# Context-mixer matrix products placed behind the expert picks on TensorE; the second tile's routing in quarters

## The chip, the core and the metric

The kernel runs on one NeuronCore of a Trainium2 chip. A core has a matrix engine (TensorE, PE in the rows; its weight loads are PEld), a vector engine (VectorE, DVE), an engine for activations (ScalarE, ACT), a general engine (GpSimd, POOL), and an engine that here only issues transfers (SyncE, SP). Each engine takes its instructions from its own queue in the order in which the compiled program put them. Transfers run on 16 DMA engines that all queues share. The metric is the device time of one launch in microseconds (us).

## The reference, cut to what matters

The input is one sequence of 256 rows of width 1024. A first block (three attention branches, then a "PEER" feed-forward) feeds a second block of two layers, each a mixer of a context (256 rows) and the latent rows, and a mixture of experts. The part around the change is the PEER feed-forward and the context's half of the second block's first mixer.

```python
q = (hf @ w_q).reshape(T, 8, 2, 128)
sc = einsum('thpd,hpkd->thpk', q, subkeys)
s1, i1 = top_k(sc[:, :, 0], 16);  s2, i2 = top_k(sc[:, :, 1], 16)
cand = s1[..., :, None] + s2[..., None, :]          # 16 x 16 per head
top_s, pos = top_k(cand, 16)                        # 16 of 16384 experts per head
gate = softmax(top_s)
act = gelu(einsum('chkd,cd->chk', u[ic], hc))       # per token 8 x 16 = 128 experts
out = einsum('chk,chkd->cd', gate * act, v[ic])
...
# second block, layer 0 (mLSTM mixer): context first, its state then feeds the latent rows
p = h_ctx @ w_in;  qk = silu(conv(p[q, k]));  v, o, gates = the rest of p
y = mlstm(q, k, v, gates);  y = norm(y) * sigmoid(o);  out_ctx = y @ w_out
```

The context's products do not depend on the PEER result, so they may run beside it.

## The kernel before

The 256 rows are two tiles of 128 tokens. `peer` (L1227) runs one phase with three strands.

- **Picks** (`picks`, L1276). For each tile, 128 picks, one for each of the 8 x 16 chosen experts; 256 in all. A pick is an indirect transfer issued by POOL (L1296) that fetches 128 rows of 8 KB (1 MB: the expert's u and v rows for every token) into one of RING = 6 buffers; a VectorE product with accumulation over 128x1024 (u times h2, through the helper at L608), and two TensorE products 128x512 in fp32 that add v, scaled by a diagonal matrix, into one accumulator. Two picks make a batch (BATCH = 2): the GELU, the product with the gate and two diagonals are made once for a batch (ACT, DVE), so TensorE gets four 128x512 products (helper `mm`, L611) for a batch. A ring buffer is free for its next pick when TensorE has read it.
- **Routing**. `prepare` (L1240) multiplies 8 slabs of `w_peer_q` for both tiles and routes tile 0 in pieces: `route(0, ...)` after slabs 0, 1, 3 and 7 (1, 1, 2 and 4 heads). `prepare_last` routes tile 1 in two pieces of four heads. `route` (L1334) is VectorE work: two rounds of maximum, index and replacement for each key list, then wide sums, comparisons and reductions over the heads of the piece.
- **Context**. `context_task` (L1519) streams 17 weight slabs (`in_w`, 1 MB each, SP, L558), each 48 products of 128x256 after a split of the slab into a high and a low part (ACT and DVE, L592 and L599), then the mixer's convolution, gates, 8 heads of attention (`mlstm_attend`, L1713), norms, output product, and the opening of the expert layer.

Emission order: `peer` chains the routing of tile 0 and then the context (with `prepare_last` woven in at a rate of 1.5) into one strand `side`. `drive` steps through the picks, and for every pick, which costs 2600, lets `side` run on for 2600 x PACE of its own cost units; a context slab costs 5200. With PACE = 0.21 a slab is emitted about every nine and a half picks. That is only the order of emission: a scheduler at build time then sets each engine's final order from the emission order and its own model of when operands are ready. `stream.shrink(2)` in `prepare` hands back two slots of the weight stream at slab 7, `stream.grow(1)` after the phase takes one again. `behind(i)` (L594) is there before: what is emitted inside it may not stand ahead of instruction `i` on that instruction's engine.

Of the kernel before, what the change touches and what calls it, by code (L numbers as in the profile page):

```python
# [23 lines left out]

PACE = 0.21

# [467 lines left out]
class K:  # L494
# [115 lines left out]
    def mm(self, ps, l, r, start=True, stop=True):  # L610
        self.nc.tensor.matmul(ps, l, r, start=start, stop=stop, skip_group_check=True)  # L611

# [614 lines left out]
    def peer(self):  # L1227
        h2, g = self.f(2048, True), self.bcast_row("ffn")
        self.ada_steps(99)
        self.mc = self.f(128, True)  # L1230
        h2T = self.norm_T([x.a for x in self.x], self.col("g_ffn"), sums=self.sq.a[:, :8], rows=(g, h2))
        self.sq.free(), g.free()
        self.mod_cols(0, [(n, b) for n in range(2) for b in range(2)])
        self.mod_cols(1, [(0, 0), (1, 0)])
        self.routes = [{"heads": 0, "rows": self.f(128), "gate": self.f(128), "act": self.f(128)} for _ in range(2)]
        side = self.chain((0.3 * c for c in self.prepare(h2T)), self.weave(self.context_task(), [self.prepare_last()], 1.5))
        self.drive(self.picks(h2, side), [side], PACE)
        self.stream.grow(1)

    def prepare(self, h2T):  # L1240
# [3 lines left out]
        for s in range(8):  # L1244
# [13 lines left out]
            p.free(), q.free()  # L1258
            yield 5200
            if s == 7:  # L1260
                for b in h2T:
                    b.free()
                sub.free()
                self.stream.shrink(2)
                self.units.lo = deque([None])
            if s in (0, 1, 3, 7):
                yield from self.route(0, {0: 0, 1: 1, 3: 2, 7: 4}[s], s + 1)

    def prepare_last(self):

        for h in (0, 4):
            yield from self.route(1, h, h + 4)
        for b in self.sc:
            self.stream.give_back(b)

    def picks(self, h2, prep):  # L1276
# [4 lines left out]
        for i, r in enumerate(self.routes):  # L1281
# [6 lines left out]
            for k in range(0, 128, BATCH):  # L1288
# [13 lines left out]
                for j, b in enumerate(got):  # L1302
# [3 lines left out]
                    for f in range(2):  # L1306
                        self.mm(po.a[:, f * 512:(f + 1) * 512], d, b[:, 1024 + f * 512:1024 + (f + 1) * 512], k + j == 0, k + j == 127)
            for f in range(2):
# [404 lines left out]
    def mlstm_attend(self, S, C):  # L1713
# [84 lines left out]

        ab = deque([alpha(0), alpha(1)])
        P = deque([weights(0, ab.popleft())])  # L1800
        for h in range(8):
            if h < 7:
                P.append(weights(h + 1, ab.popleft()))
            if h < 6:
                ab.append(alpha(h + 2))
            yield 5000 if lat else 2600
# [595 lines left out]
```

## Time and profile before

| | us |
|---|---|
| median of 3 runs (lowest, highest) | 2654.55 (2654.09, 2659.9) |
| profiled execution, its own time | 2645.13 |
| span of that execution, first to last instruction | 2643.4 |
| pick phase in it: first gather issued to last pick begun | 410.1 to about 1218 |
| mean granted TensorE clock (share of full speed) | 0.965 |

PE was busy for 87% of the span, DVE for 47%, ACT 29%, POOL 23%; the DMA engines moved 853 MB, 323 GB/s over the span. These shares are means over stages with different limits. The page's 40 slices (66 us each) show it: slices 7 to 18 are the pick phase, and in it the DMA digit stands at 9 with 405 to 420 GB/s in some slices, and at 8 or 9 with 306 to 350 GB/s in others. Rows that give busy times for chosen stretches are therefore read by stretch, each against the stretch's length. A busy number in such a row is in us; the count behind it is of recorded instructions (an fp32 product of 128x512 has two records, one of the context's 128x256 products one).

### The profile page before, as it was taken

To read this page: it belongs to the slowest core of one execution; us is meant where nothing else is said; L and a number is where in the kernel's file an instruction comes from. 1 tells how busy PE (TensorE), PEld (TensorE's weight loads), DVE (VectorE), ACT (ScalarE), POOL (GpSimd) and SP (SyncE) were. 2 spreads that over 40 slices of the span, in tenths; PEclk is the share of its full clock that TensorE was granted. 3 is DMA by queue.
4 is the path that set the end of the run, shared out by engine and by line. 5 is a ranking of instruction groups with operands and counts; after the bars stand their busy time and mean duration, and the time that the engine had idled before them with its cause. 6 is when DMAs were issued, how large, how long until landed. Compare 5 with 4: busy or idle time off the path is not lost.

```text
span 2643.4 us, 32351 instructions
## 1 busy us (share of the span) xinstructions
PE 2290.3 (87%) x12327; PEld 1386.1 (52%) x12327; DVE 1235.5 (47%) x2849; ACT 761.9 (29%) x1500; POOL 619.4 (23%) x517
## 2 busy tenths in 40 slices
PE   8999987788778897777888999999879989888876
PEld 7888985356323562225876344444469963222213
DVE  4465368899856774556774112211296451000001
ACT  6554343244513642113542000000233530000000
POOL 4233444334434433333420000000033310000000
PEclk9999998999999999999888999999979989999998
DMA  7676558888999889995456999999966389999998
GB/s 272 228 250 227 212 190 306 335 323 326 350 418 405 308 332 388 420 420 219 153 188 242 392 398 409 409 409 409 371 225 212 113 326 404 409 409 409 410 409 276
DMA packets 195323, 853.28 MB, mean 323 GB/s; under 512 B 14558, under 2 KB 39726, under 8 KB 148832
## 3 DMA queue, kind: packets, MB, share of 16 engines
q1 hardware_dynamic: 153376, 569.31, 56.6%
q0 software_dynamic: 41792, 281.90, 27.6%
q8 instruction: 97, 1.59, 0.2%
q14 instruction: 58, 0.48, 0.0%
HBM read 849.97 MB, written 1.18 MB: 322 GB/s over the span
## 4 chain that ended last, share of the span: by engine, by line
PE 49%; DMA 19%; DVE 14%; issue 8%; ACT 4%; POOL 4%; SPq 1%; POOLq 0%; DVEq 0%; ACTq 0%
PE pp L611 48%; DMA fa<-in_puv,fa 5%; DVE fa L608 5%; POOL fa L1296 3%; DMA fa<-in_moe_down 2%; ACT fa L592 2%; DMA rw<-in_moe_down 2%; DVE fa L599 2%; DMA rt<-in_moe_up 1%; DMA fa<-in_moe_up 1%; PE pp L621 1%; DMA rw<-in_moe_up 1%; DMA rw<-in_moe_gate 1%; DVE rw L599 1%; DMA fa<-in_moe_gate 1%
## 5 line engine op out<-in xcount | busy, mean ns | idle before, releaser
L611 PE MATMUL pp<-fa 128*128 128x512 f32 (+8 forms) x4900 | 1283.0, 492 | 222.7 <-ACT fa L592 157.9
L611 PEld LDWEIGHTS pp<-fa 128*128 128x128 f32 (+2 forms) x4900 | 555.7, 159 | 837.1 <-issue 432.7
L608 DVE SCALAR_TENSOR_TENSOR fa<-fa 128x1024 f32<-128x1024 f32 (+5 forms) x561 | 411.4, 756 | 166.7 <-DMA fa<-in_puv,fa 160.2
L611 PE MATMUL pp<-rw,rt 128*128 128x256 f32 x2928 | 399.9, 295 | 19.3 <-DVE rw L599 5.5
L611 PEld LDWEIGHTS pp<-rw,rt 128*128 128x128 f32 x2928 | 372.4, 197 | 42.3 <-issue 12.9
L1296 POOL DMA_INDIRECT fa<-in_puv,fa x256 | 274.3, 1072 | 450.7 <-PE pp L611 333.4
L592 ACT ACTIVATE fa<-fa 128x2 f32<-128x2 f32 (+9 forms) x477 | 189.9, 421 | 541.4 <-DVE fa L608 398.8
L611 PE MATMUL pp<-rt,rw 128*128 128x256 f32 x2448 | 327.7, 293 | 19.5 <-ACT rw L592 4.6
L611 PEld LDWEIGHTS pp<-rt,rw 128*128 128x128 f32 x2448 | 309.7, 197 | 36.5 <-issue 10.3
L599 DVE TENSOR_TENSOR fa<-pp,fa 128x512 f32<-128x512 f32 (+3 forms) x217 | 121.2, 565 | 440.3 <-PE pp L611 422.6
L592 ACT ACTIVATE fa<-pp 128x512 f32<-128x512 f32 (+4 forms) x164 | 93.8, 578 | 746.0 <-PE pp L611 586.2
L599 POOL TENSOR_TENSOR rw<-fa,rw 128x1024 fp32r<-128x1024 f32 x81 | 210.2, 2596 | 326.3 <-ACT rw L592 317.1
L592 ACT ACTIVATE rw<-fa 128x1024 fp32r<-128x1024 f32 x208 | 215.9, 1053 | 237.6 <-PE pp L611 132.2
L611 PE MATMUL pp<-rt,fa 128*64 128x512 f32 (+3 forms) x736 | 240.6, 574 | 16.1 <-DMA rt<-in_moe_up 7.8
L599 DVE TENSOR_TENSOR rw<-fa,rw 128x1024 fp32r<-128x1024 f32 x127 | 166.8, 1315 | 163.4 <-ACT rw L592 160.7
L611 PE MATMUL pp<-rw,fa 128*64 128x512 f32 (+2 forms) x720 | 202.4, 582 | 16.7 <-DMA rw<-in_moe_down 6.9
L605 DVE TENSOR_SCALAR fa<-pp,fa 128x128 f32<-128x128 f32 (+1 forms) x80 | 36.4, 460 | 254.7 <-PE pp L611 177.2
L599 DVE TENSOR_TENSOR fa<-fa 128x2 f32<-128x2 f32 (+11 forms) x325 | 99.4, 318 | 70.1 <-ACT fa L592 45.9
L611 PEld LDWEIGHTS pp<-rt,fa 128*64 128x64 f32 (+1 forms) x736 | 65.9, 124 | 118.0 <-issue 78.1
L611 PEld LDWEIGHTS pp<-rw,fa 128*64 128x64 f32 (+1 forms) x720 | 58.2, 124 | 128.8 <-issue 86.8
L621 PE MATMUL pp<-ct,fa 128*128 128x128 f32 (+3 forms) x425 | 73.7, 305 | 46.8 <-ACT fa L592 21.5
L592 ACT ACTIVATE fa<-ct,fa 128x128 f32<-128x128 f32 x256 | 88.8, 393 | 70.5 <-DVE fa L599 69.7
(136 smaller groups left out, 943.1 us busy)
## 6 DMA issues: line engine op xcount, KB each, us to landing
fa<-in_w SPq DMA_DIRECT2D x105, 1024.0 KB, 5.1
fa<-in_moe_gate SPq DMA_DIRECT2D x72, 1024.0 KB, 15.2
fa<-in_moe_down SPq DMA_DIRECT2D x68, 1024.0 KB, 14.1
fa<-in_moe_up SPq DMA_DIRECT2D x60, 1024.0 KB, 17.9
fa<-in_ada_w SPq DMA_DIRECT2D x48, 1024.0 KB, 5.4
rw<-in_moe_up SPq DMA_DIRECT2D x36, 1024.0 KB, 16.8
rt<-in_moe_down SPq DMA_DIRECT2D x31, 1024.0 KB, 13.3
rt<-in_moe_up SPq DMA_DIRECT2D x28, 1024.0 KB, 16.9
```

The source lines that it names most:

```text
L592: return self.nc.scalar.activation(out, in_, func, **kw)
L599: (eng or self.nc.vector).tensor_tensor(out, a, b, op=op)
L605: (eng or self.nc.vector).tensor_scalar(out, a, s1, s2, op0=op0, op1=op1, **kw)
L608: self.nc.vector.scalar_tensor_tensor(out, a, s, b, op0=op0, op1=op1, **kw)
L611: self.nc.tensor.matmul(ps, l, r, start=start, stop=stop, skip_group_check=True)
L621: self.nc.tensor.transpose(ps, x, self.c("ident")[:k, :k])
L1296: self.nc.gpsimd.indirect_dma_start(b, None, self.t["puv"], bass.IndirectOffsetOnAxis(ap=rows.bitcast(U32)[:, j:j + 1], axis=0))
```

## The change

1. `mm` returns its instruction. `picks` remembers in `self.pace` the last product of each batch, from the batch at which tile 0 has all its 8 heads routed, and all through tile 1. `peer` hands `drive` the generator `paced(side)`: each step of the side strand that `drive` takes is emitted inside `behind(self.pace)`, so its TensorE instructions stand behind the products of the batch they are emitted with. Other engines' queues are not bound by it.
2. `prepare_last` routes tile 1 in four pieces of two heads.
3. PACE goes from 0.21 to 0.2: a slab about every ten picks.
4. `stream.shrink(2)` moves from slab 7 to slab 3 of `prepare`.
5. `mlstm_attend`, for the context only: the decay rows (`alpha`) are fetched one head ahead instead of two, and `weights` of a head is emitted with the head itself, not one ahead. For the latent rows nothing changes (`lat` is 1).

```diff
-PACE = 0.21
+PACE = 0.2
...
     def mm(self, ps, l, r, start=True, stop=True):
-        self.nc.tensor.matmul(ps, l, r, start=start, stop=stop, skip_group_check=True)
+        return self.nc.tensor.matmul(ps, l, r, start=start, stop=stop, skip_group_check=True)
...
+        self.pace = None
         self.routes = [{"heads": 0, "rows": self.f(128), "gate": self.f(128), "act": self.f(128)} for _ in range(2)]
         side = self.chain((0.3 * c for c in self.prepare(h2T)), self.weave(self.context_task(), [self.prepare_last()], 1.5))
-        self.drive(self.picks(h2, side), [side], PACE)
+        self.drive(self.picks(h2, side), [self.paced(side)], PACE)
         self.stream.grow(1)
...
+            if s == 3:
+                self.stream.shrink(2)
             if s == 7:
                 for b in h2T:
                     b.free()
                 sub.free()
-                self.stream.shrink(2)
...
+    def paced(self, side):
+
+        while True:
+            with nullcontext() if self.pace is None else self.behind(self.pace):
+                c = next(side, None)
+            if c is None:
+                return
+            yield c
+
     def prepare_last(self):
 
-        for h in (0, 4):
-            yield from self.route(1, h, h + 4)
+        for h in range(0, 8, 2):
+            yield from self.route(1, h, h + 2)
...
                     for f in range(2):
-                        self.mm(po.a[:, f * 512:(f + 1) * 512], d, b[:, 1024 + f * 512:1024 + (f + 1) * 512], k + j == 0, k + j == 127)
+                        last = self.mm(po.a[:, f * 512:(f + 1) * 512], d, b[:, 1024 + f * 512:1024 + (f + 1) * 512], k + j == 0, k + j == 127)
+                if r is self.routes[1] or r["heads"] == 8:
+                    self.pace = last
...
-        ab = deque([alpha(0), alpha(1)])
-        P = deque([weights(0, ab.popleft())])
+        ab = deque(alpha(h) for h in range(2 if lat else 1))
+        P = deque([weights(0, ab.popleft())] if lat else [])
         for h in range(8):
-            if h < 7:
-                P.append(weights(h + 1, ab.popleft()))
-            if h < 6:
-                ab.append(alpha(h + 2))
+            if h + lat < 8:
+                P.append(weights(h + lat, ab.popleft()))
+            if h + lat < 7:
+                ab.append(alpha(h + lat + 1))
```

What this moves on the engines' queues, in the program's order. In these rows `fa 128x512` is a pick's product (two for each pick), `rw,rt 128x256` one of the context's products, `fa 128x129` and `fa 128x256` the products of an attention head, `ct,fa` a transpose; the rows of a slab's 48 products are cut here after the first or before the last few.

TensorE before, at the end of the tenth slab and in the middle of the phase:

```order
L611 MATMUL pp<-rw_71,rt_65 128x256 x2
L611 MATMUL pp<-rw_71,rt_66 128x256
L611 MATMUL pp<-fa 128x512 x4
L611 MATMUL pp<-fa 128x256 x4
L611 MATMUL pp<-fa 128x512 x6
L611 MATMUL pp<-fa 128x256 x2
L611 MATMUL pp<-fa 128x512 x6
L611 MATMUL pp<-fa 128x129 x6
L611 MATMUL pp<-fa 128x512 x112
L611 MATMUL pp<-fa 128x129 x3
```

Here 112 pick products, 56 picks, stand in one row with none of the context's between them. TensorE after, at the tenth slab and the first heads of attention:

```order
L611 MATMUL pp<-rw_69,rt_65 128x256 x2
L611 MATMUL pp<-rw_69,rt_66 128x256
L611 MATMUL pp<-fa 128x512 x20
L611 MATMUL pp<-fa 128x256 x2
L611 MATMUL pp<-fa 128x512 x8
L611 MATMUL pp<-rw_70,rt_65 128x256 x2
```

From pick 54 or so to pick 224, twenty pick products (ten picks) now stand between any two slabs, and each slab's 48 products stand together, or in two or three pieces, where before the pieces were of 2 to 93 products between batches of four pick products. The eight heads stand between picks 140 and 190 or so. The end of the phase on TensorE before:

```order
L611 MATMUL pp<-fa 16x128 x2
L611 MATMUL pp<-fa 128x512 x4
L621 MATMUL pp<-ct,fa 128x128 x2
L611 MATMUL pp<-fa 16x128 x2
L611 MATMUL pp<-fa 128x512 x184
L621 MATMUL pp<-ct,fa 128x128 x16
```

and after:

```order
L611 MATMUL pp<-fa 128x512 x4
L621 MATMUL pp<-ct,fa 128x128 x4
L611 MATMUL pp<-fa 128x512 x4
L611 MATMUL pp<-fa 16x128 x4
L611 MATMUL pp<-fa 128x512 x64
L621 MATMUL pp<-ct,fa 128x128 x16
```

The run of picks alone at the end was 184 products (92 picks) and is 64 (32 picks); the sixteen transposes behind it open the latent rows' mixer. One more place moves, far from the phase: SP's order at the start of the second layer, where `in_w` and `in_ada_w` are that layer's weights, `in_rope` and `in_dist` its tables, and `in_moe_gate` weights of its expert layer, needed much later. Before:

```order
L2226 DMA fa<-in_rope 128x640
L560 DMA fa<-in_moe_gate 128x2x1024
L2226 DMA fa<-in_dist 128x2176
L553 DMA fa<-in_moe_gate 128x1024
L558 DMA fa<-in_w 128x2048
L563 DMA fa<-in_ada_w 128x2x1024 x2
```

and after:

```order
L2239 DMA fa<-in_rope 128x640
L2239 DMA fa<-in_dist 128x2176
L558 DMA fa<-in_w 128x2048
L563 DMA fa<-in_ada_w 128x2x1024 x2
L553 DMA fa<-in_moe_gate 128x1024
```

Both `in_moe_gate` loads stood ahead of the first `in_w`; now both stand behind `in_w` and two `in_ada_w`, the 1 MB one further on.

## Rows read from the trace of the kernel before

**Rows 1.** Busy us by stretch (count), clock, DMA share, GB/s:
```profile
core 0: us, PE busy (x) PEld busy (x) DVE busy (x) ACT busy (x) POOL busy (x), PEclk, DMA share, GB/s
418.00:455.00 37.00, 30.24 (x155) 20.99 (x154) 30.90 (x104) 15.15 (x28) 13.69 (x10) 0.91 0.92 345
455.00:559.00 104.00, 78.02 (x239) 39.39 (x240) 88.24 (x332) 30.50 (x78) 38.81 (x36) 0.90 0.87 324
559.00:717.00 158.00, 136.76 (x650) 91.25 (x648) 145.36 (x388) 82.40 (x143) 67.75 (x59) 0.98 0.91 334
717.00:845.00 128.00, 94.69 (x211) 37.54 (x212) 67.69 (x132) 26.09 (x81) 50.82 (x55) 1.00 1.01 420
845.00:1004.00 159.00, 142.49 (x677) 94.73 (x677) 115.63 (x298) 83.07 (x191) 61.20 (x56) 0.95 0.87 318
1004.00:1156.00 152.00, 110.69 (x241) 43.04 (x240) 79.12 (x151) 26.98 (x90) 57.49 (x61) 1.00 1.01 419
1156.00:1219.00 63.00, 47.46 (x104) 18.27 (x102) 33.63 (x64) 10.78 (x37) 20.91 (x25) 1.00 0.97 403
```

**Rows 2.** VectorE's pick products (count) in rows 3 to 7 of that table, one answer each:
```profile
L608 DVE SCALAR_TENSOR_TENSOR fa<-fa 128x1024 f32<-128x1024 f32 x40 | 49.1, 1230 | 8.4 <-DMA fa<-in_puv,fa 8.2
...
L608 DVE SCALAR_TENSOR_TENSOR fa<-fa 128x1024 f32<-128x1024 f32 x50 | 61.2, 1225 | 51.5 <-DMA fa<-in_puv,fa 51.5
...
L608 DVE SCALAR_TENSOR_TENSOR fa<-fa 128x1024 f32<-128x1024 f32 x41 | 49.6, 1216 | 5.0 <-DMA fa<-in_puv,fa 5.0
...
L608 DVE SCALAR_TENSOR_TENSOR fa<-fa 128x1024 f32<-128x1024 f32 x61 | 74.7, 1225 | 69.8 <-DMA fa<-in_puv,fa 69.8
...
L608 DVE SCALAR_TENSOR_TENSOR fa<-fa 128x1024 f32<-128x1024 f32 x26 | 31.9, 1225 | 26.9 <-DMA fa<-in_puv,fa 26.9
```

**Rows 3.** SP's weight loads for the context, timeline of 555:700 and 855:1000:
```profile
588.27 88.38 SPq L558 DMA_DIRECT2D fa<-in_w  x9
...
863.50 124.14 SPq L558 DMA_DIRECT2D fa<-in_w  x7
```

**Rows 4.** Timeline of one batch of picks with nothing beside it:
```profile
1100.56 3.70 PE L611 MATMUL pp<-fa 128*128 128x512 f32 x8 [1.27 <-ACT fa L592]
...
1102.82 0.94 POOL L1296 DMA_INDIRECT fa<-in_puv,fa  x1 [2.32 <-PE pp L611]
```

**Rows 5.** PE in 559:717 and 845:1004 by shape, context products (count, busy us, mean ns):
```profile
L611 PE MATMUL pp<-rw,rt 128*128 128x256 f32 x240 | 31.7, 290 | 3.9 <-DVE rw L599 2.1 <-ACT rw L592 1.7
L611 PE MATMUL pp<-rt,rw 128*128 128x256 f32 x214 | 30.4, 298 | 0.3 <-ACT rw L592 0.3
...
L611 PE MATMUL pp<-rw,rt 128*128 128x256 f32 x336 | 51.6, 307 | 0.6 <-ACT rt L592 0.6
```

**Rows 6.** The same view of 400:1230, the heads' products on PE, then DVE:
```profile
L611 PE MATMUL pp<-fa 128*128 128x129 f32 x96 | 14.3, 283 | 5.5 <-ACT fa L592 3.2 <-DVE fa L608 2.3
L611 PE MATMUL pp<-fa 128*128 128x256 f32 x32 | 10.2, 456 | 5.4 <-issue 4.6 <-DVE fa L599 0.8
...
L599 DVE TENSOR_TENSOR rt<-fa,ct 128x1024 f32<-128x1024 f32 x3 | 3.7, 1223 | 0.1
L1423 DVE TENSOR_REDUCE fa<-rt 128x64 f32<-128x1024 f32 x3 | 3.6, 1216 | 0.1
...
L599 DVE TENSOR_TENSOR rt<-fa,ct 128x512 f32<-128x512 f32 x1 | 0.7, 691 | 0.0
L1423 DVE TENSOR_REDUCE fa<-rt 128x32 f32<-128x512 f32 x1 | 0.7, 686 | 0.0
```

**Rows 7.** What ended waits, by engine and line, in 559:717, 845:1004, 1005:1205:
```profile
POOL fa L1296 <- PE pp L611: 48.2, 25, 6.5
...
POOL fa L1296 <- PE pp L611: 52.4, 20, 8.5
...
DVE fa L608 <- DMA fa<-in_puv,fa: 89.6, 80, 5.0
```

**Rows 8.** Timeline of SP at the start of the second layer:
```profile
1889.58 2.87 SPq L560 DMA_DIRECT2D rt<-in_moe_down  x1
...
1899.35 0.33 SPq L558 DMA_DIRECT2D fa<-in_w  x1
```

**Rows 9.** The chain that ended last, at the same place:
```profile
1899.77 13.74 DMA fa<-in_ada_w
```

## The prediction

> **What bounds the kernel now.** First the page's slices, which place the pick phase and show that its transfer rate is not even. Then the table of busy times with the phase cut at the places where the rate changes [rows 1], and the count of picks begun in each piece [rows 2]. Read each engine's busy time against the length of its own row. Two kinds of stretch alternate. In 717 to 845 and from 1004 to 1219 there are picks and nothing else: the DMA share is 1.01, the rate 419 to 420 GB/s, and 61 picks take 152 us, 2.49 us a pick; TensorE is busy for 110.69 of 152 us and VectorE for 79.12, so neither sets the pace. A batch shows how much room TensorE has there: 3.70 us of products, then 1.27 us idle [rows 4], and VectorE's largest wait is for the gathers, 89.6 us in 200 [rows 7]. In the other kind the context and the routing run too, and DMA falls to 334 and 318 GB/s. In 559 to 717 (40 picks) VectorE is busy for 145.36 of 158 us and TensorE for 136.76: VectorE is the bound, at 8.7% over it. In 845 to 1004 (41 picks) TensorE is, with 142.49 of 159 us, 11.6% over it. There the gathers wait for TensorE to free a buffer, 48.2 and 52.4 us [rows 7].
>
> What could be won follows. A pick is 1 MB and so is a context slab, so transfers alone would need 2.49 us for each. The nine slab loads of the first mixed stretch and its 40 picks would take 122 us instead of 158, the seven of the second [rows 3] and its 41 picks 120 instead of 159. Together 75 us in which DMA has too little to do, while in the pure stretches TensorE and VectorE have.
>
> **The change part by part.** I go by picks: 0 to 40 are begun by 559 us, 40 to 80 by 717, 80 to 130 by 845, 130 to 171 by 1004, the last 85 by 1219 [rows 1, 2]. That phase is 801 us from 418. TensorE's rows after the change say where the context stands: one slab after each ten picks from pick 54 to 224, so three slabs before pick 80, six from 80 to 140, four and all eight heads from 140 to 190, four from there to 224, and 32 picks alone.
>
> Prices. Ten picks take 24.9 us of DMA, 18.5 us of TensorE (five batches of 3.70) [rows 4] and 13.0 us of VectorE (79.12 for 61 picks). A slab takes 2.49 us of DMA. On TensorE it takes 62.1 us for ten slabs in the first mixed stretch, 6.2 each, and 51.6 for seven in the second, 7.4 each [rows 5]; I take 6.8. So ten picks with a slab need 27.4 us of DMA, 25.3 us of TensorE (24.7 to 25.9) and 13.0 of VectorE with a few us of splits: DMA stays the bound, by about 2 us. The heads' products are 14.3 and 10.2 us in all, 24.5 [rows 6].
>
> VectorE's work outside the picks was 145.36 less 40 x 1.30, 93 us, in 559 to 717. By VectorE's new order, each instruction priced with the duration of its shape before, about 64 us of it (the quarters' surplus included) now stands before pick 80: some 10 us in each of the two tens up to 60, then 25 and 20. Those four tens then take 24.9 (DMA), 26.2 (DMA with a slab), 38 and 33 (VectorE): 122 us.
>
> The sum of bounds after: picks 0 to 40 as before, 37 + 104 = 141; 40 to 80, 122; 80 to 140, 66 transfers of 2.49, 164; 140 to 190, TensorE with 92.5 + 4 x 6.8 + 24.5 and some 5 of transposes, 149 (DMA would need 134); 190 to 224, 38 transfers, 95; the last 32 picks at the 2.5 us of the end before (215 us for 87), 80. That is 751, 50 below the 801.
>
> No mixed stretch before ran at its bound, so an excess comes on top. On the VectorE-bound four tens I take the 8.7% of the VectorE-bound row, 11 us; on the TensorE-bound 149 us the 11.6% of the TensorE-bound row, 17. The 259 us of DMA-bound tens with a slab have no row before. The pure stretches, also DMA-bound, have none (128 us against 50 x 2.49), the nearest mixed row 8.7%; with the room on TensorE shrunk from 6.4 us in ten picks to 2 it should lie between, and I take 4%, 10 us, since six gather buffers still let transfers queue ahead. Bounds 0 and 30. The sum is 789, **12 us less**.
>
> The smaller edits. Routing in quarters pays a wide step of 1.22 us twice as two of 0.69 [rows 6], 0.16 us more each time; six kinds of wide step, two halves, give 2 us, and the small steps of two further pieces some 4: 6 us of VectorE, inside the 64 or beside DMA-bound picks, 0 beyond what is counted; uncovered it would be 6. The heads without work one ahead cost nothing as long as a head has five picks or so, 12 us, between its weights and its values; uncovered, a head's wait stands on TensorE, at worst as long as the longest gather waits for TensorE, 8.5 us [rows 7], which is part of the excess above. PACE only sets the ten picks in a slab's spacing, counted. The earlier return of two stream slots may hold one of the last routing slabs by a load, 88.38 / 9 = 9.8 us [rows 3], or nothing; those loads have little else beside them, and I take 0.
>
> The start of the second layer: `in_w` is issued 9.8 us after the last expert load [rows 8], and the chain then waits 13.74 us on `in_ada_w` [rows 9]. 1.5 MB no longer stand ahead, 3.7 us at 2.49 per MB; a load taken from there needs its place later, where DMA idles or not. Between 0 and -3.7 I take **-2**.
>
> Together -14 on the profiled execution's 2645.13, whose span of 2643.4 leaves 1.7 us around it: 2631. The median of the runs is 9.4 above that execution, so from 2654.55 the forecast is **2640**.
>
> **The rivals.**
> *All of the excess goes* (full interleave). If the six buffers and the mixed order hide every wait, the phase is the sum of bounds, 751: -50 and -2, 2602. For it: pure stretches run at their bound. Against: no mixed row does. The Trainium skill, "Perfetto Trace Analysis" (Optimization Strategy), says that where the most-contended engine changes over time, interleaving those regimes may improve performance. By that rule the 75 us would be at stake, and the alternation of the DMA share between 1.01 and 0.87 to 0.91 agrees that there are such regimes here.
>
> *The gain is paid back* (no change). Each slab that leaves a mixed stretch makes ten pure picks take 27.4 instead of 24.9, and if the DMA-bound tens run 8% over instead of 4%, the phase is 799, with -2 to a time of 2651. For it: TensorE's room of 2 us in ten picks is a quarter of what it was.
>
> *TensorE's queue holds the picks* (slower). A slab is now one block of 6.8 us on a queue that cannot pass it, where the room between batches is 1.27 us [rows 4]. If its split is late, or the accumulator that it writes is not yet emptied, the next pick batch stands behind it, no buffer comes free, and POOL's next gather waits, as it already does for up to 8.5 us [rows 7]. At the 11.6% of the TensorE-bound row on all of the 530 us from pick 40 to 224 the phase is 751 + 61 = 812, +11 and -2, 2664; at 14%, 2676. It decides from 50 / 530, 9.4% of excess. For it: the two mixed rows before were at 8.7% and 11.6%. Against: before, too, up to 93 products stood in one piece, and those rows had two engines near their limit, while a DMA-bound ten with a slab is served by a queue filled ahead. The Trainium skill, "PSUM — Partial Sum Buffer" (Engine vs sequencer instructions), states that matmuls start and complete in program order. By it a late slab holds every pick behind it, and the order asked for here leaves no way round; by the waits of the gathers on TensorE the trace agrees.
>
> *The binding binds nothing.* The orders differ as shown, so this is left with next to nothing.
>
> **How the numbers follow.** About 0.2%, 5.3 us, is what a measurement of this kernel tells from no change. The forecast, 2628 to 2649, gets 0.44; full interleave, 2595 to 2628, 0.17; paid back, 2649 to 2660, 0.19; TensorE's queue, above 2660, 0.18; 0.02 for no binding, which is "same". Faster is 0.60 (the first two, less a little for the edge), same 0.21, slower 0.19. The range of 8 in 10 takes the middle two whole, about half of the full interleave and a third of the slow case: 2610 to 2666. The forecast's own range is 2628 to 2649.
>
> **What would show it.** Picks begun every 27 to 29 us for ten from 80 to 224, near 400 GB/s with no stretch of 100 us below 350; the last gather issued 12 us earlier, near 1197; VectorE's 93 us outside the picks no longer within 160 us. Gather waits for TensorE of 4 us and more behind each slab, with a DMA share of 0.9 all along, would show the slow rival; a share of 1.0 all along the full interleave. I am wrong if the first 40 picks move by more than 5 us, or if a strand moved behind the picks ends after them and so delays the latent rows.

## The result, and where the time went

The changed kernel takes 2692.31 us (median of 4 runs, 2689.84 to 2695.29) against 2657.23 for the kernel before (median of 4, 2654.09 to 2663.4): a ratio of 1.013, 95% interval 1.0106 to 1.0153. It is 35 us slower, where 14 less had been forecast.

The profiled execution of the changed kernel has a span of 2688.1 us, that of the kernel before 2643.4. The 44.7 us between them are more than the 35 between the medians, because the profiled execution of before is 12 us quicker than the median of its runs, that of after 2.5 us. The pick phase is best cut at the issues of the gathers, whose records are complete (256 in each trace). From the first to the last issue it is 798.9 us before and 833.7 after, 34.8 more; the first gather is issued 4.6 us later (414.7 against 410.1), and from the last gather to the end of the span it is 1439.8 instead of 1434.4, 5.4 more.

The table of busy times of the changed kernel, cut at the issues of gathers 40, 80, 140, 190, 224 and 255 (columns as in [rows 1]):

```profile
551.50:684.90 133.40, 98.55 (x321) 51.18 (x320) 117.80 (x412) 45.73 (x96) 55.80 (x49) 0.91 0.84 321
684.90:875.40 190.50, 154.74 (x537) 83.37 (x536) 112.97 (x231) 65.26 (x134) 77.68 (x67) 0.93 0.93 368
875.40:1058.20 182.80, 147.83 (x534) 84.25 (x533) 120.47 (x296) 72.98 (x182) 71.78 (x73) 0.90 0.91 335
1058.20:1161.90 103.70, 90.41 (x340) 49.73 (x339) 55.07 (x104) 26.34 (x74) 38.67 (x34) 0.97 0.92 368
1161.90:1248.30 86.40, 65.30 (x184) 29.63 (x182) 46.54 (x99) 22.41 (x61) 36.27 (x32) 0.98 0.97 392
```

And the kernel before, cut at the same gathers:

```profile
553.10:709.10 156.00, 137.56 (x660) 92.78 (x659) 147.23 (x403) 82.42 (x142) 67.53 (x59) 0.97 0.90 326
709.10:873.50 164.40, 124.81 (x335) 55.82 (x334) 98.68 (x205) 43.40 (x122) 65.47 (x68) 0.99 1.00 407
873.50:1047.40 173.90, 148.33 (x631) 90.28 (x630) 110.84 (x274) 74.26 (x177) 66.11 (x61) 0.96 0.90 338
1047.40:1132.70 85.30, 62.97 (x138) 24.46 (x137) 44.67 (x85) 15.24 (x51) 32.45 (x35) 1.00 1.01 420
1132.70:1209.00 76.30, 56.93 (x124) 21.91 (x122) 40.61 (x77) 13.53 (x45) 29.04 (x31) 1.00 1.01 420
```

Row against row: 40 to 80 is 23 us shorter, as the slabs have left it. 80 to 140 is 26 longer, 140 to 190 is 9 longer although it holds four slabs instead of six (it now holds all of the heads' products, though, where before had less than half of them there, as the lines further down show), 190 to 224 is 18 longer and 224 to 255 is 10 longer. From 80 to 224 no engine fills a row of after: in 80 to 140 TensorE is busy for 154.74 of 190.5 us, VectorE for 112.97, and the DMA share is 0.93 at 368 GB/s. No row of after has the share of 1.01 and the 419 to 420 GB/s of [rows 1]; only gathers 230 to 250 still take 25.0 and 24.9 us for ten. TensorE's granted clock, 0.96 to 1.00 in the rows of before, is 0.90 to 0.98 in those of after.

What a slab does there repeats every ten picks, 30 to 36 us. One such turn on the timeline of the changed kernel (TensorE, VectorE and POOL; start, length, what, idle before and what ended it):

```profile
832.33 6.31 PE L611 MATMUL pp<-rw,rt 128*128 128x256 f32 x48
...
833.17 1.96 POOL L1307 DMA_INDIRECT fa<-in_puv,fa  x1 [0.53 <-PE pp L611]
...
838.49 10.69 PE L611 MATMUL pp<-fa 128*128 128x512 f32 x24
...
840.64 1.65 POOL L1307 DMA_INDIRECT fa<-in_puv,fa  x1 [5.51 <-PE pp L611]
...
848.89 1.22 DVE L608 SCALAR_TENSOR_TENSOR fa<-fa 128x1024 f32<-128x1024 f32 x1 [4.60 <-DMA fa<-in_puv,fa]
...
853.58 2.07 PE L611 MATMUL pp<-fa 128*128 128x512 f32 x2 [4.41 <-ACT fa L592]
```

While TensorE is on the 48 products (6.31 us) it reads no gather buffer, so none is freed beyond what the picks ahead of the block had freed, and GpSimd waits 5.51 us before it can issue the next gather. Behind 13 of the 17 slabs it is idle for 4.5 us or more before a gather. DMA runs short. The 24 records behind the block are six picks, a whole ring, read in one go, and the gathers that refill them are issued close together, from 840.64 on. VectorE waits 4.60 us, to 848.89, for the first of them, and TensorE is idle for 4.41 us behind it. After that idle time the next two records of pick products take 2.07 us, 1.03 each, where eight take 3.70 in [rows 4]: the lower of TensorE's two clock levels, 1.2 GHz. The same turn in slices of 8 us (columns as above): the DMA share falls to 0.64 at 239 GB/s behind the block, the clock to 0.57 after the idle time.

```profile
828.00:836.00 8.00, 8.00 (x39) 5.31 (x38) 4.29 (x8) 0.98 (x4) 4.08 (x3) 0.95 1.01 419
836.00:844.00 8.00, 8.00 (x36) 4.82 (x35) 5.64 (x9) 3.49 (x7) 2.59 (x2) 1.00 0.64 239
844.00:852.00 8.00, 5.18 (x13) 1.96 (x11) 3.23 (x6) 0.79 (x3) 4.28 (x4) 1.00 1.01 426
852.00:860.00 8.00, 6.42 (x8) 2.69 (x9) 4.30 (x9) 1.86 (x6) 0.94 (x1) 0.57 1.01 425
```

What ended waits in gathers 80 to 140 (total, times, longest), the kernel before and then the changed one:

```profile
POOL fa L1296 <- PE pp L611: 77.5, 47, 2.6
DVE fa L608 <- DMA fa<-in_puv,fa: 54.9, 52, 1.8
...
PE pp L611 <- ACT fa L592: 38.8, 28, 3.5
```
```profile
POOL fa L1307 <- PE pp L611: 64.7, 32, 6.5
DVE fa L608 <- DMA fa<-in_puv,fa: 54.3, 36, 4.6
...
PE pp L611 <- ACT fa L592: 35.8, 17, 4.4
POOL fa L1307 <- DVE fa L608: 26.8, 8, 6.7
```

Gathers wait for TensorE, VectorE for gathers, and TensorE (through ScalarE's diagonals) for VectorE, in both kernels, and the totals of these three have not grown. What changed is their shape: fewer waits, and longer ones, 6.5 us where the longest was 2.6. With waits of up to 2.6 us the DMA share of this stretch was 1.00; behind the wait of 5.51 us in the turn above it is 0.64.

### The profile page after: what moved, and what is told of

Its sections match the earlier page's. It is cut to its first block, busy times and chain, and to the rows that moved or that the text cites. A ratio compares the mean times of both kernels' runs of the same rounds, so it can differ in the third digit from the quotient of the medians.

```text
span 2688.1 us, 32433 instructions
## 1 busy us (share of the span) xinstructions
PE 2310.7 (86%) x12327; PEld 1393.6 (52%) x12327; DVE 1238.5 (46%) x2901; ACT 762.3 (28%) x1503; POOL 635.1 (24%) x517
## 4 chain that ended last, share of the span: by engine, by line
PE 46%; DMA 24%; DVE 15%; issue 7%; ACT 4%; POOL 3%; SPq 1%; POOLq 0%; DVEq 0%; ACTq 0%
PE pp L611 44%; DMA fa<-in_puv,fa 9%; DVE fa L608 6%; DMA fa<-in_moe_down 3%; ACT fa L592 2%; DMA rw<-in_moe_down 2%; POOL fa L1307 2%; DVE fa L599 2%; DVE rw L599 2%; DMA fa<-in_moe_up 1%; DMA rw<-in_moe_up 1%; DMA rt<-in_moe_up 1%; DMA rw<-in_moe_gate 1%; DMA fa<-in_moe_gate 1%; ACT rw L592 1%
## 5 line engine op out<-in xcount | busy, mean ns | idle before, releaser
L611 PE MATMUL pp<-fa 128*128 128x512 f32 (+8 forms) x4900 | 1307.8, 501 | 251.2 <-ACT fa L592 186.4
L611 PEld LDWEIGHTS pp<-fa 128*128 128x128 f32 (+2 forms) x4900 | 567.8, 162 | 883.0 <-issue 466.2
L608 DVE SCALAR_TENSOR_TENSOR fa<-fa 128x1024 f32<-128x1024 f32 (+4 forms) x563 | 410.3, 752 | 198.6 <-DMA fa<-in_puv,fa 186.8
L611 PE MATMUL pp<-rw,rt 128*128 128x256 f32 x2928 | 390.0, 291 | 16.5 <-DVE fa L608 6.2
L1307 POOL DMA_INDIRECT fa<-in_puv,fa x256 | 292.8, 1144 | 417.1 <-PE pp L611 276.2
L611 PEld LDWEIGHTS pp<-rw,rt 128*128 128x128 f32 x2928 | 366.7, 195 | 35.8 <-issue 11.8
L592 ACT ACTIVATE fa<-fa 128x128 f32<-128x128 f32 (+7 forms) x479 | 189.1, 420 | 547.6 <-DVE fa L608 400.5
L611 PE MATMUL pp<-rt,fa 128*64 128x512 f32 (+3 forms) x736 | 240.6, 574 | 14.3 <-DMA rt<-in_moe_up 7.8
L599 DVE TENSOR_TENSOR fa<-fa 128x2 f32<-128x2 f32 (+11 forms) x353 | 106.0, 313 | 71.5 <-ACT fa L592 45.9
L621 PE MATMUL pp<-ct,fa 128*128 128x128 f32 (+3 forms) x425 | 71.4, 301 | 54.2 <-ACT fa L592 28.5
## 6 DMA issues: line engine op xcount, KB each, us to landing
rt<-in_moe_down SPq DMA_DIRECT2D x31, 1024.0 KB, 13.6
```

The source lines that it names most:

```text
L592: return self.nc.scalar.activation(out, in_, func, **kw)
L599: (eng or self.nc.vector).tensor_tensor(out, a, b, op=op)
L608: self.nc.vector.scalar_tensor_tensor(out, a, s, b, op0=op0, op1=op1, **kw)
L611: return self.nc.tensor.matmul(ps, l, r, start=start, stop=stop, skip_group_check=True)
L621: self.nc.tensor.transpose(ps, x, self.c("ident")[:k, :k])
L1307: self.nc.gpsimd.indirect_dma_start(b, None, self.t["puv"], bass.IndirectOffsetOnAxis(ap=rows.bitcast(U32)[:, j:j + 1], axis=0))
```

## The experiments

All times of stretches below are from the issue of one gather to that of another in the profiled execution, in us; "rest" is from the last gather to the end of the span. The first stretch to look at is the phase, since the rest differs between builds by up to 29 us for a reason of its own (last section).

| kernel | 0-40 | 40-140 | 140-255 | phase | rest | ratio to before (interval) |
|---|---|---|---|---|---|---|
| before | 143.0 | 320.4 | 335.4 | 798.9 | 1434.4 | 1 |
| changed | 136.8 | 323.9 | 372.9 | 833.7 | 1439.8 | 1.013 (1.0106 to 1.0153) |
| no_bind | 137.2 | 340.9 | 326.0 | 804.1 | 1438.3 | 1.0008 (0.9992 to 1.0025) |
| bind_only | 141.6 | 330.2 | 367.0 | 838.8 | 1434.3 | 1.0112 (1.0083 to 1.0141) |
| parts2 | 137.0 | 324.8 | 366.8 | 828.5 | 1443.9 | 1.0105 (1.0077 to 1.0133) |
| parts4 | 136.8 | 321.1 | 380.4 | 838.3 | 1446.3 | 1.0139 (1.0114 to 1.0165) |
| bind_all | 129.6 | 316.7 | 368.5 | 814.7 | 1438.0 | 1.0055 (1.0032 to 1.0079) |
| all_parts4 | 129.4 | 302.9 | 365.7 | 798.0 | 1454.7 | 1.0041 (1.0021 to 1.006) |
| ring7 | 132.6 | 314.3 | 356.6 | 803.5 | 1445.5 | 1.0018 (1.0004 to 1.0032) |
| ring7_before | 139.4 | 308.9 | 338.2 | 786.4 | 1463.5 | 1.0064 (1.0038 to 1.0089) |
| ring7_all_parts4 | 130.2 | 295.2 | 350.1 | 775.5 | 1451.0 | 0.9952 (0.9935 to 0.997) |
| ring7_all_cut | 129.9 | 294.6 | 350.4 | 774.7 | 1448.3 | 0.9941 (0.9922 to 0.9959) |

**Which part of the change: the binding or the rest.** `no_bind` is the changed kernel without the binding.

```diff
-                if r is self.routes[1] or r["heads"] == 8:
-                    self.pace = last
```

> The changed kernel with self.pace left at None, so that no step is bound behind the picks; quarters, PACE 0.2, the earlier shrink and the shorter lookahead stay. Theory (the binding, which makes 48-product blocks between batches of picks): the pick phase returns to 795 to 810 us from 836, time 2650 to 2668. Rival (the other edits cost the time): phase 830 or more, time 2685 to 2695.

Measured: 2659.99 us against 2660.13 for the kernel before beside it, ratio 1.0008 with 1 inside its interval; phase 804.1. So quarters, PACE, the earlier shrink and the shorter lookahead together cost nothing that can be measured in the total. By stretches they do move time: 40 to 140 is 20 us longer than before, 0 to 40 and 140 to 255 are 6 and 9 shorter. Set against this kernel, the binding gains 17 us in 40 to 140 and loses 47 in 140 to 255. `bind_only` is the other half, the kernel before with `mm` returning its instruction, `paced`, and `self.pace = last`, nothing else.

> The kernel before with the binding alone; halves, PACE 0.21, shrink at slab 7 and the old lookahead stay. Theory (the binding): phase 825 to 850, time 2680 to 2705. Rival (the other edits): phase 795 to 810, time 2650 to 2665.

Measured: 2687.42, ratio 1.0112; phase 838.8, rest 1434.3 as before. The binding alone makes the loss, all of it in the pick phase, and both figures lie where the theory had them.

**Is it the length of the block? Inside the changed kernel.** `parts2` and `parts4` let the context's slabs of qk, v and norm be emitted in two or four steps, with the cost of the slab divided among them (nine slabs, those of qk and v, really stand apart on TensorE, those of norm mostly not):

```diff
-            p = self.slab_T(S["hT"], w)
+            p = (yield from self.steps(S["hT"], w, False)) if seg else self.slab_T(S["hT"], w)
...
+    def steps(self, hT, w, row, parts=4):
+        p, k = self.ps(), 0
+        for a in range(2):
+            for c in range(8):
...
+                self.mm3(p.a[:, a * 256:(a + 1) * 256], x, y, c == 0, c == 7)
+                k += 1
+                if k % (16 // parts) == 0 and k < 16:
+                    yield 5200 // parts
+        return p
```

> The changed kernel with the nine slabs of qk and v emitted in two steps of 24 products, half the cost each, so that a bound block on TensorE is 3.2 us instead of 6.3; the eight slabs of norm and out stay whole (norm's are stepped too, but mostly stand as 48). Theory (block length against the room of six gather buffers): tens of picks from 54 to 140 fall from 31.5 us towards 29, phase 815 to 828, time 2668 to 2682. Rival (a slab's transfer beside the gathers costs it, or the other edits): unchanged, 2688 to 2696.

> The same with four steps of 12 products, 1.6 us each, one behind nearly every batch. Theory (block length): tens of picks from 54 to 140 at 27.4 to 28.5 us, phase 805 to 820, time 2660 to 2675, and TensorE's granted clock in that stretch above 0.95. Rival (transfer beside the gathers, or the other edits): unchanged, 2688 to 2696.

Measured: 2684.1 (1.0105) and 2694.64 (1.0139). Gathers 80 to 140 take 190.0 and 194.5 us, against 190.5 in the changed kernel, and the granted clock there is 0.91 in `parts4`, where above 0.95 was expected. Cutting the block alone gains nothing that can be told from the changed kernel's 1.013, and the theory's expectation fell for both.

**Is it the length of the block? Where there are picks and nothing else.** Seven more 128x512 products of TensorE for ten picks (6.2 us, no transfer, no split, result unused) were put into the stretch of the kernel before in which picks run alone, once as one block and once cut into one or two behind each batch, with (1, 2, 1, 2, 1) in the first line of the diff. These two were run once each, for the trace (2685.77 and 2660.22 us, beside a median of 2654.68 for the kernel before).

```diff
+                n = (0, 0, 0, 0, 7)[k // 2 % 5]
+                if i == 1 and k >= 50 and n:
+                    p = self.ps()
+                    with self.behind(last):
+                        for _ in range(n):
+                            self.mm(p.a, ident, h2.a[:, :512])
+                    p.free()
```

> The kernel before, with seven more 128x512 fp32 products on TensorE (6.5 us, no transfer, no split, result unused) in one block behind every fifth batch of the second tile from pick 178 on, where before there are picks alone at 24.9 us for ten. Theory A (block length): 29 to 31 us for ten. Theory B (a loop of six buffers with little slack: TensorE's time is paid in full, however it is cut): 30 to 31.5. Theory C (the slab's transfer costs the time): 24.9 to 25.5.

> The same seven products for ten picks, cut into one or two behind each batch. Theory A (block length): TensorE's own 18.5 + 6.5 = 25.0, so 25 to 26.5 us for ten. Theory B (paid in full): 29.5 to 31.5. Theory C (transfer): 24.9 to 25.5.

Gathers 220 to 250 of the kernel before, of the block and of the spread (columns as above). Earlier gathers are left out because in the spread build the context's work itself moved: its 140 to 190 is 12 us shorter than before and its 190 to 224 is 14 longer.

```profile
1122.70:1197.40 74.70, 55.57 (x122) 21.59 (x121) 39.42 (x75) 13.53 (x45) 28.14 (x31) 1.00 1.01 420
```
```profile
1138.40:1224.00 85.60, 75.79 (x164) 32.18 (x163) 40.52 (x76) 13.53 (x45) 32.78 (x30) 0.94 0.93 371
```
```profile
1130.70:1206.40 75.70, 71.93 (x164) 30.02 (x163) 39.47 (x75) 13.45 (x45) 28.48 (x31) 1.00 1.01 421
```

The same 42 further records cost 10.9 us as three blocks, 3.6 us each, and 1.0 us spread out. That is 28.5 and 25.2 us for ten picks, against 24.9: the spread is where theory A had it, the block half a microsecond below its 29 to 31. With the block the DMA share is 0.93 and the clock 0.94, spread 1.01 and 1.00. The timeline of the block (TensorE and POOL) has the same picture as a slab of the changed kernel, without a slab's transfer or split:

```profile
1172.74 6.17 PE L611 MATMUL pp<-fa,ct 128*128 128x512 f32 x14
...
1180.91 0.94 POOL L1296 DMA_INDIRECT fa<-in_puv,fa  x1 [6.79 <-PE pp L611]
...
1192.18 8.83 PE L611 MATMUL pp<-fa 128*128 128x512 f32 x16 [2.52 <-ACT fa L592]
```

So the block's length does count, without any transfer of a slab: an idle-looking TensorE (18.5 of 24.9 us) can give 5.5 us in ten picks away (71.93 less 55.57, over three tens) for 0.3 us if they are cut small, but not in one piece.

**Why cutting the slabs did not help.** The timeline of `parts4` shows what still holds the picks (ScalarE, VectorE and TensorE):

```profile
777.73 1.99 PE L611 MATMUL pp<-rw,rt 128*128 128x256 f32 x12
...
779.76 1.06 ACT L592 ACTIVATE rw<-fa 128x1024 fp32r<-128x1024 f32 x1 [4.93 <-PE pp L611]
780.85 1.23 DVE L599 TENSOR_TENSOR rw<-fa,rw 128x1024 fp32r<-128x1024 f32 x1 [4.69 <-ACT rw L592]
781.99 1.22 DVE L608 SCALAR_TENSOR_TENSOR fa<-fa 128x1024 f32<-128x1024 f32 x1
...
784.56 2.07 PE L611 MATMUL pp<-fa 128*128 128x512 f32 x2 [4.84 <-ACT fa L592]
```

The split of a later piece (ScalarE, `rw<-fa`) waits 4.93 us for the bound products on TensorE to free the buffer that it writes. On VectorE the second half of the split stands ahead of the next pick's product and waits 4.69 us for ScalarE; the pick's data had landed, since its product starts without a wait of its own at 781.99. TensorE, which needs that pick, is idle for 4.84 us. The binding set TensorE's order only; ScalarE's and VectorE's still followed the scheduler's own idea of when a buffer comes free. `bind_all` binds each side step on these two engines as well:

```diff
-            with nullcontext() if self.pace is None else self.behind(self.pace):
+            with ExitStack() as es:
+                for x in self.pace or ():
+                    es.enter_context(self.behind(x))
                 c = next(side, None)
...
-                    self.pace = last
+                    self.pace = (last, diag, gated)
```

> The changed kernel with each side step bound on ScalarE and VectorE too (behind the batch's last diagonal and its gate product), so that a split of the next slab no longer stands in these queues ahead of picks it could follow. Theory D (the split, held by a register that TensorE's bound block has not freed, holds the picks' GELU and products behind it): phase 800 to 815, time 2655 to 2672. Theory B (loop of six buffers): phase 825 to 845, time 2680 to 2700.

Measured: 2666.98, ratio 1.0055, phase 814.7, both within theory D's ranges, the phase at their upper end. But it did not come from where theory D had it: gathers 80 to 140 stay at 192.6 us. Its gain is 16.5 us in 0 to 80 (253.7 against 270.2), where VectorE has less to do, as tile 1's routing stands later on it (VectorE is busy for 143.91 us in 80 to 140, in the changed kernel for 112.97), and 7 in 140 to 190 (175.7 against 182.7), less 5 elsewhere. With whole blocks, order on the other two engines does not mend the stretch of the slabs.

`all_parts4` does both, four steps and three engines.

> The changed kernel bound on TensorE, ScalarE and VectorE, with the slabs of qk, v and (in part) norm cut into four steps of 12 products: both edits that alone left the gathers 80 to 140 at 190 us or more (190.5 in the changed kernel, 192.6 bound on three engines, 194.5 in four steps). Theory A+D (either a whole block on TensorE or a split standing ahead of picks on ScalarE and VectorE is enough to hold them): gathers 80 to 140 in 165 to 174 us, time 2640 to 2655. Rival (neither; the six buffers are too few for a slab beside picks however it is placed): 186 to 195 us, time 2665 to 2680.

Measured: 2668.46, ratio 1.0041, and a phase of 798.0, 36 us below the changed kernel's. The total lies in the rival's range and not in that of theory A+D, but the rest, which neither theory was about, had grown by 20 us. Gathers 80 to 140 took 180.9, outside either range. The rows of that stretch for `parts4`, `bind_all` and `all_parts4`:

```profile
677.30:871.90 194.60, 156.55 (x538) 86.43 (x537) 120.81 (x285) 66.57 (x138) 75.01 (x69) 0.91 0.93 361
```
```profile
668.30:860.90 192.60, 155.17 (x538) 84.29 (x537) 143.91 (x410) 62.52 (x131) 72.91 (x66) 0.93 0.92 362
```
```profile
664.50:845.40 180.90, 150.10 (x538) 83.45 (x537) 141.12 (x383) 61.84 (x129) 71.57 (x63) 0.96 0.97 386
```

The DMA share is 0.97 only with both, and this although 20 to 28 us more of VectorE's work stand in the stretch than in `parts4` and the changed kernel. That the routing moves between stretches is why the table sums gathers 40 to 140: 323.9 changed, 321.1 in four steps, 316.7 on three engines, 302.9 with both. The 3 and 7 us of one edit alone become 21 together. Each figure is from one profiled execution; the two `extra` builds, whose edit begins at pick 178, took 323.3 and 323.9 us for gathers 40 to 140 where the kernel before took 320.4, so 3 us tells nothing, 7 little, and 21 is well clear. So either a whole block on TensorE or a split out of step on ScalarE and VectorE was enough to hold the picks here. The expected 165 to 174 us left out that the transfers themselves keep the DMA engines busy for longer there: 0.97 of 180.9 is 175 us, at 386 GB/s, where picks alone run at 420 with 1.01. What slows them was not tried.

**The room that the ring of buffers gives.** `ring7` is the changed kernel with a seventh gather buffer from the moment tile 0 is routed, and one slot of the weight stream less for it.

```diff
+                if len(ring) < 7 and self.wide and self.FA.room() >= 2048:
+                    ring.append(self.f(2048, True))
                 got = []
...
                 sub.free()
+                self.stream.shrink(1)
+                self.wide = True
...
-        self.stream.grow(1)
+        self.stream.grow(2)
```

> The changed kernel with a seventh gather buffer from the moment tile 0 is routed (one weight-stream slot less for the phase in exchange). Theory B (loop of six buffers): tens from pick 80 to 224 fall from 31 to 28 or 29 us, phase 800 to 818, time 2655 to 2675. Rival (order of the splits on ScalarE and VectorE): unchanged within 5 us, 2685 to 2697.

Measured: 2661.81, ratio 1.0018, phase 803.5: of the 35 us by which the changed kernel's phase is longer, one more buffer, 2.49 us of transfers, gives 30 back. In 80 to 140 it is only 7.5 us (183.0), in 140 to 190 it is 12.7 (170.0), and ten picks from 80 to 224 fell from 33.1 to 31.6 us, not to 28 or 29: phase and time came as theory B had them, the tens did not. The rest is 5.7 us longer. `ring7_all_parts4` joins all three edits, and `ring7_before` is the kernel before with the seventh buffer alone.

> The same with a seventh gather buffer once tile 0 is routed. Theory A+D: gathers 80 to 140 in 164 to 168 us (66 transfers at 2.49 are 164), time 2632 to 2648. Rival (six buffers too few): 175 to 183, as the seventh buffer alone gave 183.0, time 2650 to 2660.

> The kernel before with the seventh gather buffer, nothing else. If a seventh buffer helps wherever TensorE holds the picks, the stretch of seven slabs and eight heads (gathers 140 to 190, 173.9 us) falls to 160 to 167 and the time to 2638 to 2648; where picks are alone nothing changes, 2.49 us each. If the buffer only mends what the binding broke: 2652 to 2660.

`ring7_all_parts4` takes 2639.37, ratio 0.9952 (0.9935 to 0.997): half a percent below the kernel before, and below the changed one, in the time that theory A+D had. Its phase is 775.5, 23 us below that of before, and 17 us of this are given back in the rest. Gathers 80 to 140 at 176.2 again miss 164 to 168 and lie in the rival's 175 to 183, but with a DMA share of 0.99 at 394 GB/s: now the DMA engines are busy nearly all along, and the held gathers leave little of their time unused. `ring7_before` is slower, 2669.77 (1.0064): its phase gains 12.5 us, none of it in 140 to 190 (174.3 against 173.9), and its rest loses 29. Both of its expectations fell. The buffer gives 12.5 us without the binding and 30 with it, so more than half of what it gave was mending what the binding broke.

Last, `ring7_all_cut` cuts three of the output product's four slabs too, which stood whole behind the picks after gather 190.

```diff
-                p = self.slab_row(yT, w, tiles=tiles)
+                p = (yield from self.steps(yT, w, True)) if eng and n == 2 else self.slab_row(yT, w, tiles=tiles)
...
-            yield 5200
+            yield 1300 if eng and k < 3 else 5200
```

> The kernel bound on three engines, slabs in four steps, seven buffers, with three of the four slabs of the output product cut into four steps too, which stood whole behind the picks in gathers 190 to 255. Theory A+D: gathers 190 to 224 fall from 92.8 to 87 to 91 us, and 224 to 255 from 82.7 to 77 to 81; time 2628 to 2638. Rival (a whole block costs nothing once there are seven buffers): both unchanged within 2 us, time 2636 to 2643.

Measured: 2638.76, ratio 0.9941 (0.9922 to 0.9959); 92.6 and 82.7 us where 92.8 and 82.7 were. With seven buffers and three engines bound, those whole blocks cost nothing more; 34 picks and three slabs at 2.49 us are 92.1, so the first of the two stretches was at its DMA bound already. The rival was right here.

## Why the prediction was wrong

- **The first 40 picks** were taken as unchanged. They took 136.8 us instead of 143.0, from a first gather 4.6 us later; `no_bind` has the same 137.2, so it is one of the smaller edits, and all but 1.6 us cancels itself. The prediction had named a move of more than 5 us there as a sign that it is wrong.
- **40 to 80** was put at 122 of bound and 11 of excess, 133. Measured 133.4, in tens of 25.7, 31.5, 38.9 and 37.3 us where the bounds were 24.9, 26.2, 38 and 33. VectorE was busy for 117.80 us, 65.8 of it outside the picks, where 64 had been read off its order. The price list and that reading were right; the sum hit more closely than its parts. The second ten, the DMA-bound one with a slab, ran 20% over (15% by the price list's own 27.4, which the 26.2 falls short of), and this was the case still to come.
- **The step that failed is the excess on the DMA-bound tens with a slab.** It was taken at 4% between 0 (pure picks) and 8.7% (nearest mixed row), "since six gather buffers still let transfers queue ahead", 10 us on 259. Measured: 190.5 and 103.8, 294.3 us, 13.6%. The bounds of 0 and 30 us were given, and 35 came: 25 of the some 47 us by which the phase missed its forecast. The lower bound of 0 was a misreading already: 717 to 845 took 128 us for 50 picks, 2.8% over their 124.5. The argument compared sums: 25.3 us of TensorE fit into 27.4 us of DMA. It needed the shape: one 6.3 us piece against what the ring holds in reserve. The block without a slab costs 3.6 us; by that price, an estimate, six blocks are 22 of the 26 us by which 80 to 140 went over its bound of 164. They were not the only cause: with the blocks cut but the splits left out of step it stayed at 194.5, and with both mended 9.6 us came back, 14.3 with the seventh buffer too. TensorE's room of 2 us in ten picks, called a quarter of what it was, is a third of 6.4.
- **The TensorE-bound stretch**, 140 to 190, was put at 149 plus 11.6%, 166. TensorE was busy for 147.83, close to the price, but by luck in part: the picks' products took 107.8 us at a granted clock of 0.90 where 92.5 was priced, slabs, heads and transposes 48.4 where 57 was. The stretch took 182.7, 23% over. It has the same long turns, with heads' products between the picks on top; how the 34 us divide between slabs and heads was not measured.
- **The end**: 224 to 255 took 86.4 where 80 was put and 76.3 was before. Cut at the gathers, the last slab stands in it (it begins 0.9 us after gather 224).
- **The second layer** was put at -2 for two loads that no longer stand ahead of `in_w`. The whole rest came out at +5.4. `in_w` now follows `in_rope` by 8.71 us, before by 6.81, so no gain from the freed place shows. From `in_rope` to the end it is 756.6 us after and 750.8 before, but `bind_only` and the `extra` builds, with the old order, have 753.4 to 763.7: the term is too small to be read here. Before, then after:

```profile
1892.54 2.86 SPq L2226 DMA_DIRECT2D fa<-in_rope  x1
```
```profile
1931.47 2.87 SPq L2239 DMA_DIRECT2D fa<-in_rope  x1
...
1940.18 0.33 SPq L558 DMA_DIRECT2D fa<-in_w  x1
```

- **The rivals.** "TensorE's queue holds the picks" had 0.18. It had the mechanism with its place and its price, named the sign that came (gather waits of 4 us and more behind slabs; the DMA share is 0.91 to 0.97 from pick 80 on), and said that it decides from 9.4% of excess on the 530 us from 40 to 224. Measured there: 610.4 us, 15%. It even listed 14%, 2676. It was argued down by the pieces of up to 93 products that before held; but nearly all of the slabs stood where VectorE or TensorE was the bound and DMA had slack. Its guess at the cause, a late split, is only half of it: the block holds the picks without any split (`extra_block`). The chance was wrong because both mixed rows, 8.7 and 11.6%, lay on either side of the break-even and the new case was put below both.
- **Paid back** is right as bookkeeping for 40 to 140, 320.4 and 323.9 us. The loss stands in 140 to 255, 37.5 us. Before had a heap there, and then picks at 2.49 each. The groups on TensorE in gathers 140 to 190, before and after (count, busy us):

```profile
L611 PE MATMUL pp<-rw,rt 128*128 128x256 f32 x288 | 45.1, 309 | 0.6 <-ACT rt L592 0.6
L611 PE MATMUL pp<-fa 128*128 128x129 f32 x54 | 8.0, 281 | 3.5 <-ACT fa L592 3.2 <-DVE fa L608 0.3
...
L611 PE MATMUL pp<-fa 128*128 128x256 f32 x8 | 2.1, 379 | 0.0
```
```profile
L611 PE MATMUL pp<-rw,rt 128*128 128x256 f32 x192 | 25.6, 292 | 0.0
L611 PE MATMUL pp<-fa 128*128 128x129 f32 x96 | 12.0, 275 | 0.0
L611 PE MATMUL pp<-fa 128*128 128x256 f32 x32 | 8.4, 380 | 0.0
```

  Cut at gather 140, the heap was six slabs (288 products) and 10.1 us of the heads' products; with 12.8 us of transposes and small products that is 68 us of TensorE's work beside the picks of 140 to 255. After has 85 there: eight slabs (50.8), all heads (20.4) and 13.7 of the rest. Picks alone would take 115 x 2.49 = 286, so the heap cost 49 us and the even spread 87. The heap's first slab and 5.5 us more of heads' products stand in the ten gathers ahead of 140; with these ten it is 63 us for 81 before, and 93 for 91 after. So part of the loss is only that more work stands there. The other part is the price: 1.0 us for each us of TensorE's work spread out in whole blocks, 0.7 to 0.8 in the heap.
- Where the prediction weighed the rule of the Trainium skill, "Perfetto Trace Analysis" (Optimization Strategy), that interleaving regimes may improve performance: the runs bear it out with a condition. The regimes were interleaved by the binding and the phase became 35 us longer; it became 23 us shorter than before when the pieces were small, the queues of three engines agreed and there was a buffer more (the buffer alone gave the kernel before 12.5 of it). The rule of the Trainium skill, "PSUM — Partial Sum Buffer" (Engine vs sequencer instructions), that matmuls start and complete in program order, agrees with the held gather of 5.51 us in the turn shown, which was issued only when TensorE had come through the block to its picks. No run here tests the rule itself.

## What to carry to other kernels

Work that fits by its sum beside a saturated transfer loop may still not fit by its pieces: compare the longest piece on the in-order engine with the reserve of the ring, here 6.3 us against six buffers of 2.49 us that circulate with little to spare. Where an order is forced on one engine, look at the queues of the engines that feed it: here they waited for it with the picks' work behind them, and small pieces paid only once these queues were bound too. A heap of side work where another engine is the bound can be cheaper than an even spread. Read waits by their length, and not only by their total.

## What was not expected of the hardware

- **The clock follows the pattern, and is the smaller part.** TensorE fell to the lower level after idle times of some 4 us behind a held gather (1.03 us a record instead of 0.46). In gathers 80 to 140 the same 241 recorded pick products took 113.6 us at a granted clock of 0.99 before and 121.0 at 0.93 after:

```profile
L611 PE MATMUL pp<-fa 128*128 128x512 f32 x241 | 113.6, 614 | 38.8 <-ACT fa L592 38.8
```
```profile
L611 PE MATMUL pp<-fa 128*128 128x512 f32 x241 | 121.0, 653 | 35.8 <-ACT fa L592 35.8
```

  That is 7 us more of busy TensorE where the stretch is 26 us longer; how much of the 7 stands on the path was not measured.
- **The second layer answers to the first.** The rest after the pick phase differs between builds by 0 to 29 us, although the sources differ only before it, and nearly all of it falls after `in_rope`: from the last gather to there it is 680 to 685 us in every build, from there to the end 751 to 779. In `ring7_before` (779) SP's order there has other neighbours, and between two `in_ada_w` loads nothing but one `in_moe_gate` is issued for 22 us:

```profile
1914.69 0.37 SPq L563 DMA_DIRECT2D fa<-in_ada_w  x1
1915.11 0.61 SPq L560 DMA_DIRECT2D fa<-in_moe_gate  x1
1936.89 0.37 SPq L563 DMA_DIRECT2D fa<-in_ada_w  x1
```

  What sets that order was not tried, and the order at this place is not all: `extra_block` keeps that of before and has 764. With the rest of the kernel before, `ring7_all_cut` would be 14 us faster still; that is arithmetic, not a run.
